# Feed-forward in seven block products twice: the second product inside the next group's first, chunk operands built in the background through DRAM

## The chip, the cores and the metric

One core of one Trainium2 chip runs the whole program. The time is the device time of one execution in microseconds; the number that counts is the median of the runs. PE is the matmul engine (PEld its weight loads), DVE the vector engine, ACT the scalar engine, POOL the GpSimd engine, SP the engine that issues most DMAs.

## What is computed

One encoder layer over 2048 + 256 tokens of 1024 channels, in float32: a mixing part (windowed attention, a Fourier mix, memory attention) that ends in an output projection with a residual add, then a squared-ReLU MLP and a final norm.

```python
    x = x + group_output_norm(y_attn, y_four, y_mem, g_grp) @ w_out
    hf = rmsnorm(x, g_ffn) @ w_ff1                      # 1024 -> 4096
    x = x + jnp.square(jax.nn.relu(hf)) @ w_ff2         # 4096 -> 1024
    ...
    return rmsnorm(x, g_final)
```

## The kernel before

Every product in float32 is done as three matmuls on reduced operands: an operand `a` is cut into a high part (`hi_of`, an ACT copy, L101) and a low part (`lo_of`, a subtraction, L104, on DVE unless POOL is named), and high x high, high x low and low x high are added up in PSUM. So each operand tile costs one ACT and one DVE (or POOL) instruction before PE can use it.

The stages follow one another: input projection (to 345 us of the profile), mixing with the output projection (to about 800 us), feed-forward (to the end). The code writes each engine's instructions in program order; a scheduler that simulates the kernel then fixes the order on every engine, with priority to what was written first, and assigns the buffers. On the chip each engine runs its list strictly in that order.

*Mixing.* 18 blocks of 128 tokens. `outproj` of a block is two halves (`op_b_0`, `op_b_1`) of 24 matmuls 512 wide through the one bank of the pool `ps_p`, each followed by a DVE add into the tile `xr`, and a store of the tile to DRAM (`X2d`). `drain(5)` lets five matmuls of it be written between the pieces of attention.

*Feed-forward.* The 2304 tokens are cut into 3 chunks of 768 (`CH`), the 4096 hidden channels into 16 groups `j` of two tiles of 128. In a group, the first product (weights `w1` x tokens `XT`) is cut into 2 x 2 blocks and done with Strassen's seven products: each (`pr`) is 12 matmuls 384 wide. Sums of weight blocks (`as`) are made on POOL, five per group, each weight operand is split by ACT and DVE (`w1h`, `w1l`), and the seven results are joined into four quarters of the hidden values (`post`: ACT copies, POOL sums, DVE adds). A DVE instruction takes the square of the ReLU, ACT and DVE split the quarter (`hh`, `hl`). The second product is plain: `slices` makes 12 pieces of 6 matmuls 512 wide (`y`), each added on DVE to `acc`. The pieces of group j - 1 are written between the products of group j (`EVEN`). ACT and POOL split `w2` (`w2h`, `w2l`).

*Chunk start.* The right operands of the seven products, `XT` (seven combinations of token halves and channel halves, high and low, one buffer), are made by `build`: it loads the mixing's result, norms it (`norm_tile`), transposes it on PE (`tf`, 48 per chunk), scales, sums and splits it. For chunks 1 and 2 this stands between the last group's `y` pieces (`tail`), after the old chunk's last `pr`; the final norm of the old chunk (`final`, L1113) runs beside the first products of the new one. Raw tiles come through a ring of 12 (`granule`).

## Time and profile before

| | |
|---|---|
| median of 3 runs | 2394.8 us (2394.55 to 2401.86) |
| profiled execution, span | 2396.3 us |
| PE busy | 2295.1 us, 12896 matmuls |
| DVE / ACT / POOL busy | 1642.2 / 1038.0 / 1035.3 us |
| DMA moved | 237.93 MB, mean 99 GB/s |

The profiled execution's own time is its span; it lies 1.5 us above the median. In the profile's groups a row gives line, engine, operation, output and inputs, shape, count, then busy time and mean duration of one, then the engine's idle time just before and what ended it. A matmul's printed duration includes its way through the pipeline, so how often PE can start one is read from neighbouring start times.

### The profile page before, as it was taken

How to read it: one execution, taken by the hardware profiler on the slowest of the kernel's cores; microseconds unless marked ns; L12 is line 12 of the kernel's file. 1: busy time of each engine (PE TensorE's matmuls, PEld its weight loads, DVE VectorE, ACT ScalarE, POOL GpSimd, SP SyncE). 2: the span in 40 equal slices, each digit the busy share in tenths (PEclk: the TensorE clock that was granted, in tenths of full speed). 3: DMA queues.
4: the chain of work that ended last, by engine and by line, in shares of the span. 5: the costliest groups of instructions: out<-in, count | busy, mean ns of one | idle time of the engine just before them, and what ended most of it. 6: DMA issues, size and time to landing. Idle time of an engine off the chain costs nothing.

```text
span 2396.3 us, 35759 instructions
## 1 busy us (share of the span) xinstructions
PE 2295.1 (96%) x12896; PEld 2072.1 (86%) x12896; DVE 1642.2 (69%) x2910; ACT 1038.0 (43%) x2406; POOL 1035.3 (43%) x1001
## 2 busy tenths in 40 slices
PE   7999978999999799999998899999998899999998
PEld 7999977888888689899996789999996789899996
DVE  6333558777666876766666996666667986666666
ACT  6433357676667633333334533233335533333333
POOL 1100130000001965555555864555556865555544
PEclk9999989999999899999999999999999999999999
DMA  7343275243333522222221432222221532222211
GB/s 245 115 146 97 72 243 211 93 143 102 111 106 102 185 71 63 70 71 71 67 66 45 159 128 67 66 71 67 71 71 53 176 106 66 71 71 67 65 50 53
DMA packets 120777, 237.93 MB, mean 99 GB/s; under 512 B 11927, under 2 KB 35479, under 8 KB 120343
## 3 DMA queue, kind: packets, MB, share of 16 engines
q1 hardware_dynamic: 111648, 219.82, 28.6%
q10 hardware_dynamic: 7191, 12.80, 1.5%
q0 software_dynamic: 1760, 3.02, 0.5%
q8 instruction: 102, 1.67, 0.3%
q14 instruction: 76, 0.62, 0.1%
HBM read 189.98 MB, written 46.53 MB: 99 GB/s over the span
## 4 chain that ended last, share of the span: by engine, by line
PE 69%; DVE 7%; POOL 4%; issue 3%; DMA 1%; ACT 1%; POOLq 0%; SPq 0%; DVEq 0%; ACTq 0%
PE y L98 27%; PE pr L98 25%; PE op L98 8%; PE ot L98 2%; PE s L98 2%; PE t L646 2%; DVE acc L1113 1%; DVE XTl L104 1%; DVE acc L295 1%; POOL w2l L104 1%; POOL as L1008 1%; DMA wos<-in_w_out_dram 1%; DVE hl L104 1%; DVE w1l L104 1%; PE sm L98 1%
## 5 line engine op out<-in xcount | busy, mean ns | idle before, releaser
L295 DVE TENSOR_TENSOR acc<-acc,y 128x512 f32<-128x512 f32 x576 | 388.8, 680 | 169.6 <-PE y L98 165.8
L98 PE MATMUL pr<-XTh,w1h 128*128 128x384 f32 x1344 | 458.1, 342 | 22.9 <-ACT w1h L101 9.7
L98 PE MATMUL y<-w2h,hh 128*128 128x512 f32 x1152 | 454.4, 394 | 20.8 <-DVE acc L295 20.7
L98 PE MATMUL pr<-XTh,w1l 128*128 128x384 f32 x1344 | 455.9, 340 | 11.5 <-DVE w1l L104 11.4
L98 PE MATMUL pr<-XTl,w1h 128*128 128x384 f32 x1344 | 456.0, 339 | 1.0 <-DVE XTl L104 1.0
L98 PE MATMUL y<-w2h,hl 128*128 128x512 f32 x1152 | 449.2, 390 | 0.7 <-DVE hl L104 0.7
L98 PE MATMUL y<-w2l,hh 128*128 128x512 f32 x1152 | 449.8, 390 | 0.0
L1008 POOL TENSOR_TENSOR as<-w,w 128x512 f32<-128x512 f32 x240 | 345.8, 1448 | 208.1 <-DVE w1l L104 171.6
L104 POOL TENSOR_TENSOR w2l<-w,w2h 128x512 fp32r<-128x512 f32 x192 | 268.9, 1422 | 365.0 <-ACT w2h L101 365.0
L101 ACT ACTIVATE w1h<-as 128x512 fp32r<-128x512 f32 x240 | 151.8, 633 | 521.5 <-PE pr L98 496.4
L104 DVE TENSOR_TENSOR w1l<-as,w1h 128x512 fp32r<-128x512 f32 x240 | 219.8, 916 | 121.4 <-ACT w1h L101 121.2
L98 PEld LDWEIGHTS pr<-XTh,w1h 128*128 128x128 f32 x1344 | 255.6, 190 | 42.0 <-ACT w1h L101 12.3
L98 PEld LDWEIGHTS pr<-XTh,w1l 128*128 128x128 f32 x1344 | 255.4, 190 | 18.9 <-DVE w1l L104 14.3
L98 PEld LDWEIGHTS y<-w2h,hh 128*128 128x128 f32 x1152 | 217.0, 188 | 59.7 <-DVE acc L295 21.6
L98 PEld LDWEIGHTS pr<-XTl,w1h 128*128 128x128 f32 x1344 | 255.7, 190 | 14.3 <-DVE XTl L104 1.7
L98 PEld LDWEIGHTS y<-w2h,hl 128*128 128x128 f32 x1152 | 216.9, 188 | 47.6 <-DVE hl L104 1.3
L98 PEld LDWEIGHTS y<-w2l,hh 128*128 128x128 f32 x1152 | 217.2, 189 | 28.8
L98 PE MATMUL pj<-hl_x,winh 128*128 128x256 f32 x720 | 204.1, 285 | 0.8 <-DVE hl_x L104 0.8
L98 PE MATMUL pj<-hh_x,winl 128*128 128x256 f32 x720 | 204.0, 284 | 0.0
L98 PE MATMUL pj<-hh_x,winh 128*128 128x256 f32 x720 | 202.9, 286 | 0.6 <-ACT hh_x L101 0.6
L127 POOL TENSOR_SCALAR stats<-stats 128x1 f32<-128x1 f32 x36 | 8.6, 239 | 394.9 <-ACT jk L747 394.9
L101 ACT ACTIVATE w2h<-w 128x512 fp32r<-128x512 f32 x192 | 119.2, 624 | 77.7 <-PE y L98 42.8
(209 smaller groups left out, 4269.6 us busy)
## 6 DMA issues: line engine op xcount, KB each, us to landing
w<-in_w_dram SPq DMA_DIRECT2D x384, 256.0 KB, 2.8
qb<-Qd SPq DMA_DIRECT2D x18, 768.0 KB, 7.4
Qd<-q SPq DMA_DIRECT2D x24, 512.0 KB, 2.8
x<-in_x_dram SPq DMA_DIRECT2D x18, 512.0 KB, 4.5
xr<-in_x_dram SPq DMA_DIRECT2D x18, 512.0 KB, 4.2
X2d<-xr SPq DMA_DIRECT2D x18, 512.0 KB, 3.1
xs<-X2d SPq DMA_DIRECT2D x36, 256.0 KB, 3.4
acc<-X2d SPq DMA_DIRECT2D x18, 512.0 KB, 5.6
```

Of the source, the lines that this page charges most:

```text
L98: pe.matmul(out, lhsT, rhs, start=start, stop=stop)
L101: act.activation(out, src, AF.Copy, scale=scale)
L104: (eng or dve).tensor_tensor(out=out, in0=src, in1=hi.bitcast(F32), op=ALU.subtract)
L127: pool.tensor_scalar(out=st, in0=st, scalar1=1.0 / width, scalar2=EPS, op0=ALU.mult, op1=ALU.add)
L295: TT(out=o, in0=a, in1=b, op=ALU.add)
L646: pe.transpose(t[:, j], p[:, j * P:(j + 1) * P], ident)
L1008: pool.tensor_tensor(out=t, in0=raw[c, j, a[0]], in1=raw[c, j, a[1]], op=a[2])
L1113: dve.scalar_tensor_tensor(out=o, in0=o, scalar=st[:, 0:1], in1=gf[n], op0=ALU.mult, op1=ALU.mult)
```

## The change

- Both products of the feed-forward are now seven block products of Winograd's form, in which sums are shared. The first keeps 7 x 12 matmuls 384 wide per group, but pairs of products add up in the same PSUM bank (`pa` to `pd`), so the results come out with fewer joins. The second works on two groups at once (`g`, halves `e`): `half_step` is 9 matmuls 512 wide, 14 of them per pair of groups (63 per group instead of 72). Its results are kept in 21 accumulators, one set for each product, which are joined only at the end of a chunk (`finish`).
- One half step is written after each product, 14 steps (`LAG`) behind: the second product of a pair of groups runs inside the first products of the next pair.
- The activations' combinations are summed on POOL (`sumA`, 4 per group) and split on ACT and DVE (`splitA`, 7 per group). The combinations of `w2` are made once, in the projection stage, on POOL with loads from POOL's own queue, and stored to DRAM (`w2_sums`, `W2T`); those of `w1` are made in chunk 0 and stored (`W1S`), and loaded again in the other chunks.
- The norm ahead of the feed-forward and its transposes go into `outproj`: behind the two `op` halves of a block come two squares on ACT, the root on POOL, one DVE scaling, and twice four transposes (`xp`) through the same one-bank pool `ps_p` with a DVE multiply each. The result goes to DRAM (`XnT`). `drain(5)` becomes `drain(6)`.
- Chunk 0's operands are built while the last blocks finish. Those of chunks 1 and 2 are built during the chunk before (`build_next`: 6 units of 8 steps, one step per product, from the third group on: 4 POOL sums, 7 ACT copies and 7 DVE subtractions of 256 elements and 14 stores per unit) and stored (`XD`). Each of the seven is loaded (`load_x`, two tiles of 0.79 MB) after the last product that reads the old one.
- The ring of raw tiles grows to 16.

```diff
+        def w2_sums():
...
+                        pool.dma_start(t, w2[2 * j + k].rearrange("p (n c) -> p n c", n=2)[:, :, qs])
...
+                    minus(t[:, 0], b[0][:, 1], b[0][:, 0])
+                    minus(t[:, 1], b[1][:, 1], t[:, 0])
+                    minus(b[0][:, 1], b[1][:, 1], b[0][:, 1])
+                    minus(b[1][:, 0], t[:, 1], b[1][:, 0])
+                    sp.dma_start(W2T[j][:, 1:3, qs], t)
+                    sp.dma_start(W2T[j][:, 3, qs], b[0][:, 1])
+                    sp.dma_start(W2T[j][:, 0, qs], b[1][:, 0])
...
             sp.dma_start(X2d[b], xt)
+            st = op.tile([P, 2], F32, tag="xst", bufs=2, name=f"xst_{b}")
+            for n in range(2):
+                jk = op.tile([P, 512], BF16, tag="xjk", bufs=1, name=f"xjk{n}_{b}")
+                act.activation(jk, xt[:, n * 512:(n + 1) * 512], AF.Square, scale=D ** -0.5, accum_out=st[:, n:n + 1])
+            rstd_of_means(st)
+            dve.tensor_scalar(out=xt, in0=xt, scalar1=st[:, 0:1], scalar2=None, op0=ALU.mult)
+            xv = xt.rearrange("p (k t) -> p k t", k=KT)
+            for n in range(2):
+                ps = ps_p.tile([P, 4, P], F32, tag="p", name=f"xp_{b}_{n}")
+                ks = slice(4 * n, 4 * n + 4)
+                for k in range(4):
+                    pe.transpose(ps[:, k], xv[:, 4 * n + k], ident)
+                    yield
+                TT(out=xv[:, ks], in0=ps, in1=gain[:, 3, ks].unsqueeze(2).to_broadcast([P, 4, P]), op=ALU.mult)
+            sp.dma_start(XnT[b], xv)
...
-            drain(5)
+            drain(6)
...
+        ORD1 = (1, 6, 2, 7, 5, 4, 3)
+        ORD2 = (1, 2, 4, 5, 6, 7, 3)
...
+        steps1 = [(c, j, i) for c in range(NCH) for j in range(NJ) for i in ORD1]
+        steps2 = [(c, g, i, e) for c in range(NCH) for g in range(NG) for i in ORD2 for e in range(2)]
+        PER = 7 * NJ
+        LAG = 14
...
+        def build_next(c):
+            for i in range(NT):
+                for kp in range(2):
+                    def put(n, src, i=i, kp=kp):
+                        t = late[0].tile([P, 2, 2, P], F32R, tag="raw", bufs=NRAW, name=f"xd_{c}_{i}_{kp}_{n}")
+                        hi_of(t[:, 0], src)
+                        lo_of(t[:, 1], src, t[:, 0])
+                        dst = XD[c, n].rearrange("q p k t -> p q k t")
+                        for q in range(2):
+                            sp.dma_start(dst[:, q, 2 * kp:2 * kp + 2, i * P:(i + 1) * P].bitcast(F32), t[:, q].bitcast(F32))
+                    yield from x_unit(c, i, kp, put)
+
+        def load_x(c, i):
+            for q, t in enumerate(xt_tiles(c, i)):
+                sp.dma_start(t.bitcast(F32), XD[c, i][q].bitcast(F32))
...
+        def half_step(r):
+            c, g, i, e = steps2[r]
...
+            for t in range(NT):
+                if e == 0:
+                    ybank[t] = ps_y.tile([P, 512], F32, tag="y", bufs=4, name=f"y_{c}_{g}_{i}_{t}")
+                ps = ybank[t]
+                ts_ = slice(t * P, (t + 1) * P)
+                mm(ps, ah[:, ts_], wh, e == 0, False)
+                mm(ps, ah[:, ts_], wl, False, False)
+                mm(ps, al[:, ts_], wh, False, e == 1)
+                if e == 1:
+                    if (c, i, t) not in acc:
+                        acc[c, i, t] = acc_tile(c, i, t)
+                        act.activation(acc[c, i, t], ps, AF.Copy)
+                    else:
+                        (sub if i == 4 else add)(acc[c, i, t], acc[c, i, t], ps)
...
+        for n in range(len(steps1) + LAG):
+            r = n - LAG
...
+            load1(n + 5)
+            load2(r + 4)
+            load_acc(r + 3)
+            split1(n + 2)
+            split2(r + 2)
+            splitA(r + 2)
+            sumA(r + 4)
+            if n < len(steps1):
+                product(n)
+                c, j, i = steps1[n]
+                if j == NJ - 1 and c + 1 < NCH:
+                    load_x(c + 1, i)
+                if n % PER == 16 and c + 1 < NCH:
+                    background = build_next(c + 1)
+                if background is not None:
+                    next(background, None)
+            if r >= 0:
+                half_step(r)
+                c, g, i, e = steps2[r]
+                if pending:
+                    pending.pop(0)()
+                if g == NG - 1 and e == 1:
+                    pending += finish(c, i)
```

How the lists of the engines change is seen at three places. A row is the engine's next instruction: line, operation, output<-inputs, width, and the engines or queues that it waits for.

DVE in the mixing, behind the add of the second `op` half of block 4 (the first row of each). Around it stand instructions of the next blocks' attention: `ptl`, `pml`, `ytl` are low parts, `p` and `stats` belong to the softmax. Before:

```order
L295 TENSOR_TENSOR xr_4_5961<-xr_4_5961,op_4_1_6061 128x512 [waits PE_49]
L104 TENSOR_TENSOR ytl_5_0_6174<-ty_5_0_6168,yth_5_0_6173 128x512 [waits Activation_49]
L637 TENSOR_REDUCE stats_6_5341<-sm_6_2_6152 128x1 [waits PE_49]
L104 TENSOR_TENSOR ytl_5_1_6183<-ty_5_1_6177,yth_5_1_6182 128x512 [waits Activation_49]
L637 TENSOR_REDUCE stats_6_5341<-sm_6_3_6191 128x1 [waits PE_49]
L104 TENSOR_TENSOR ptl_6_4_6144<-t_6_6_6201,pth_6_4_6143 128x3x128 [waits Activation_49]
```

Now:

```order
L326 TENSOR_TENSOR xr_4_6463<-xr_4_6463,op_4_1_6563 128x512 [waits PE_49]
L659 ISA p_7_0_6759,stats_7_5804<-s_7_0_6756,bias_4722,nsink_313 128x384 [waits PE_49]
L659 ISA stats_7_5804 128x1
L676 TENSOR_REDUCE stats_7_5804<-sm_6_3_6715 128x1 [waits Activation_49]
L724 RECIPROCAL stats_6_5801<-stats_6_5801 128x4
L105 TENSOR_TENSOR ptl_6_4_6653<-t_6_7_6762,pth_6_4_6652 128x3x128 [waits Activation_49]
L659 ISA p_7_1_6786,stats_7_5804<-s_7_1_6783,bias_4722,nsink_313 128x384 [waits PE_49]
L659 ISA stats_7_5804 128x1
L105 TENSOR_TENSOR pml_6_0_6795<-tm_6_0_6789,pmh_6_0_6794 128x512 [waits Activation_49]
L105 TENSOR_TENSOR pml_6_1_6816<-tm_6_1_6810,pmh_6_1_6815 128x512 [waits Activation_49]
L837 TENSOR_SCALAR xr_4_6463<-xr_4_6463,xst_4_6698 128x1024 [waits DMAHW7_49,DVE_49,Pool_49]
```

The scaling of block 4 (last row) is new; nine instructions of other work stand between the add and it, and it waits for POOL and for a DMA (the store of the tile to `X2d`).

PE in the same place, where `sm` and `s` are attention scores, `t` and `o` transposes and `otm` an attention output. Before, the matmuls behind the last of `op_4_1`:

```order
L98 MATMUL op_4_1_6061<-woh_7_4335,ytl_4_1_5958 128x512
L757 MATMUL ty_5_0_6168<-ident_60,y_5_5882 128x128 [waits DVE_49,PE_49]
L757 MATMUL ty_5_0_6168<-ident_60,y_5_5882 128x128 x3
L757 MATMUL ty_5_1_6177<-ident_60,y_5_5882 128x128 [waits DMAHW1_49,PE_49]
L757 MATMUL ty_5_1_6177<-ident_60,y_5_5882 128x128 x3
L98 MATMUL sm_6_2_6152<-km_0_4325,qb_6_5338 128x256 [waits Activation_49]
```

Now, around the second four transposes of block 4:

```order
L99 MATMUL otm_6_2_6939<-pmh_6_3_6872,vm_0_4745 128x256
L843 MATMUL xp_4_1_6712<-ident_60,xr_4_6463 128x128 [waits DVE_49]
L843 MATMUL xp_4_1_6712<-ident_60,xr_4_6463 128x128 x3
L99 MATMUL otm_6_2_6939<-pml_6_3_6873,vm_0_4745 128x256 [waits DVE_49]
L99 MATMUL otm_6_2_6939<-pmh_6_3_6872,vm_0_4745 128x256
```

The transposes stand in PE's list and wait there for DVE; everything behind them waits too.

PE at the first chunk boundary, before, where the old chunk's last `y` pieces and the new chunk's first `pr` alternate:

```order
L98 MATMUL y_0_15_0_1_14826<-w2h_0_15_1_0_14528,hh_0_15_0_14637 128x512 [waits DVE_49]
L98 MATMUL y_0_15_0_1_14826<-w2l_0_15_1_0_14529,hh_0_15_0_14637 128x512 [waits Pool_49]
L98 MATMUL y_0_15_0_1_14826<-w2h_0_15_1_0_14528,hl_0_15_0_14638 128x512
L98 MATMUL y_0_15_0_1_14826<-w2h_0_15_1_1_14532,hh_0_15_2_14368 128x512
L98 MATMUL y_0_15_0_1_14826<-w2l_0_15_1_1_14533,hh_0_15_2_14368 128x512 [waits Pool_49]
L98 MATMUL y_0_15_0_1_14826<-w2h_0_15_1_1_14532,hl_0_15_2_14369 128x512
L98 MATMUL pr_1_0_1_14937<-XTh_1_14469,w1h_1_0_1_14919 128x384 [waits Activation_49]
```

Now:

```order
L99 MATMUL pc_0_15_15476<-XTh3_0_10363,w1h_0_15_3_15464 128x384
L99 MATMUL pc_0_15_15476<-XTl3_0_10364,w1h_0_15_3_15464 128x384
L99 MATMUL pc_0_15_15476<-XTh3_0_10363,w1l_0_15_3_15465 128x384
L99 MATMUL y_0_6_3_0_15542<-w2h_0_6_3_1_15468,ah_0_6_3_1_15472 128x512 [waits Activation_49]
L99 MATMUL y_0_6_3_0_15542<-w2l_0_6_3_1_15469,ah_0_6_3_1_15472 128x512 [waits Pool_49]
L99 MATMUL y_0_6_3_0_15542<-w2h_0_6_3_1_15468,al_0_6_3_1_15473 128x512
L99 MATMUL y_0_6_3_1_15546<-w2h_0_6_3_1_15468,ah_0_6_3_1_15472 128x512
L99 MATMUL y_0_6_3_1_15546<-w2l_0_6_3_1_15469,ah_0_6_3_1_15472 128x512
L99 MATMUL y_0_6_3_1_15546<-w2h_0_6_3_1_15468,al_0_6_3_1_15473 128x512
L99 MATMUL y_0_6_3_2_15550<-w2h_0_6_3_1_15468,ah_0_6_3_1_15472 128x512
L99 MATMUL y_0_6_3_2_15550<-w2l_0_6_3_1_15469,ah_0_6_3_1_15472 128x512
```

No transpose stands there any more: the first product of chunk 1 (`pa_1_0`) follows 9 `y` matmuls behind the last product of chunk 0 (`pc_0_15`), and what it waits for is the DMA that brings its operand.

549 lines of the change are left out of this document (276 added, 273 removed).

## Prediction

> **What bounds the kernel now.** I read the profile page first (shares of the engines, the chain that ended last), then a table of busy times by stage, then the timeline of single matmuls, then the groups of instructions of an undisturbed stretch of the feed-forward.
>
> ```profile
> span 2396.3 us, 35759 instructions
> PE 2295.1 (96%) x12896; PEld 2072.1 (86%) x12896; DVE 1642.2 (69%) x2910; ACT 1038.0 (43%) x2406; POOL 1035.3 (43%) x1001
> PE 69%; DVE 7%; POOL 4%; issue 3%; DMA 1%; ACT 1%; POOLq 0%; SPq 0%; DVEq 0%; ACTq 0%
> ```
>
> The matmul engine is busy for 96% of the span and holds 69% of the chain, so matmuls taken away count nearly in full, and whatever makes PE wait counts in full too. The stages, in the order PE, PEld, DVE, ACT, POOL (busy us and instructions), clock, DMA share, GB/s:
>
> ```profile
> 345.00:772.00 427.00, 414.09 (x2448) 358.08 (x2447) 305.59 (x884) 295.92 (x869) 27.69 (x71) 0.99 0.37 128
> 1280.00:1400.00 120.00, 100.45 (x461) 84.40 (x460) 106.68 (x142) 59.65 (x138) 88.12 (x97) 0.91 0.40 134
> 1400.00:1800.00 400.00, 399.23 (x2016) 362.50 (x2014) 274.22 (x401) 129.68 (x238) 223.43 (x172) 1.00 0.22 68
> 1800.00:1940.00 140.00, 121.67 (x589) 103.31 (x590) 123.45 (x169) 67.97 (x153) 104.58 (x110) 0.96 0.37 122
> 1940.00:1960.00 20.00, 20.00 (x105) 18.39 (x104) 17.73 (x23) 7.31 (x15) 10.73 (x9) 1.00 0.30 85
> ```
>
> The mixing (345 to 772) has PE at 97%. Inside a chunk (1400 to 1800) PE never rests while DVE is 69% busy; for 20 us it even holds with DVE at 89%. At the two chunk boundaries (1280 and 1800), where the next chunk's operands are built, DVE is the full engine, 106.68 of 120 us, and PE loses time.
>
> Next the start times of neighbouring matmuls, 384 wide (pr), then 512 wide (y), and eight transposes:
>
> ```profile
> 818.24 0.34 PE L98 MATMUL pr<-XTh,w1h 128*128 128x384 f32 x1
> ...
> 818.77 0.34 PE L98 MATMUL pr<-XTh,w1h 128*128 128x384 f32 x1
> 2352.17 0.39 PE L98 MATMUL y<-w2h,hl 128*128 128x512 f32 x1
> ...
> 2352.85 0.39 PE L98 MATMUL y<-w2h,hl 128*128 128x512 f32 x1
> 781.56 1.03 PE L936 MATMUL tf<-ident,xs 128*128 128x128 f32 x8
> ```
>
> Three steps each: (818.77 - 818.24)/3 = 0.177 us and (2352.85 - 2352.17)/3 = 0.227 us. A group (two ff tiles of one chunk) is 84 pr and 72 y: 31.2 us, 0.200 us per matmul.
>
> **The change, part by part.** *Removed matmuls.* The second product takes 63 instead of 72 y matmuls in each of 48 groups: 432 x 0.227 = **-98 us**; a group is then 29.1 us. pr stays at 84. 144 tf transposes go and 144 xp come, at 0.13 us each: zero, though 96 of them move from the boundaries into the mixing.
>
> *Boundaries.* Of 461 matmuls in 1280 to 1400, 48 are tf (6 us) and 413 x 0.200 = 83 us the rest: 31 of 120 us were lost. For 1800 to 1940 (589): 108 + 6, 26 lost. Together 57. The new order puts the next chunk's first product directly behind the last one of the old, so this loss goes; what is late next is the finish of the chunk. It adds 12 POOL adds, 12 DVE adds and 12 DVE scalings in the 14 half steps (58 us) that end a chunk:
>
> ```profile
> L295 DVE TENSOR_TENSOR acc<-acc,y 128x512 f32<-128x512 f32 x151 | 101.9, 680 | 44.7 <-PE y L98 43.6
> L1008 POOL TENSOR_TENSOR as<-w,w 128x512 f32<-128x512 f32 x64 | 89.8, 1410 | 60.9 <-DVE w1l L104 57.0 <-DMA w<-in_w_dram 3.7
> L104 POOL TENSOR_TENSOR w2l<-w,w2h 128x512 fp32r<-128x512 f32 x50 | 68.4, 1389 | 109.4 <-ACT w2h L101 109.4
> L104 DVE TENSOR_TENSOR w1l<-as,w1h 128x512 fp32r<-128x512 f32 x67 | 59.9, 894 | 38.1 <-ACT w1h L101 38.1
> L104 DVE TENSOR_TENSOR hl<-m,hh 128x384 fp32r<-128x384 f32 x36 | 33.8, 938 | 1.2 <-ACT hh L101 1.2
> L295 DVE TENSOR_TENSOR m<-m,pr 128x384 f32<-128x384 f32 x39 | 20.4, 545 | 2.1 <-PE pr L98 1.6 <-POOL md L1055 0.5
> L1055 POOL TENSOR_TENSOR mx<-mx,m 128x384 f32<-128x384 f32 x13 | 18.1, 1392 | 0.9
> L1113 DVE SCALAR_TENSOR_TENSOR acc<-acc,ff,gf 128x512 f32<-128x512 f32 x12 | 17.7, 1518 | 0.8 <-POOL ff L132 0.8
> ```
>
> (The last row is from 1280 to 1400.) DVE: 12 x 0.894 + 12 x 1.518 = 29 us on top of two groups. The two groups alone cost DVE 46 us (next paragraph), so 75 us of work meet 58 us of matmuls. I take 14 us lost per boundary, nearly the excess of 17, because some scalings run on into the next group; bounds 0 (all of them do) and 28 (the loss of before). Term: -57 + 28 = **-29**.
>
> *DVE and POOL inside the groups.* Before, 12.8 groups in the 400 us: 21.4 us of DVE each. Now per group 9.75 instead of 12 adds of y (the rest goes to ACT as copies or vanishes), -1.5; 7 instead of 4 low halves of the activations (384 wide, 0.94), +2.8; five instead of four adds of pr, +0.5. That is 23.2 of 29.1 us, 80%. The background build adds 42 low halves of 256 elements to some 7 groups of each of the first two chunks, at about 0.6 (half to two thirds of the 512 wide row): +3.6, 92%. POOL: 7 x 1.39 for w2l and 4 x 1.39 for sums of the activations, 15 us; in chunk 0 four weight sums (1.41) more, 21 us, 72%. At 89% DVE the old kernel lost nothing, at 89% with POOL at 73% it lost a quarter. I take 2 us for each of chunk 0's seven groups with the build, 3 in its rest, 4 in chunk 1: **+21**, bounds 0 and 65 (16% of 14 groups, the lost share of 1280 to 1400).
>
> The reason it could be more is that DVE and POOL hinder each other:
>
> ```profile
> 1510.65 0.69 DVE L104 TENSOR_TENSOR w1l<-w,w1h 128x512 fp32r<-128x512 f32 x1 [0.33 <-ACT w1h L101]
> 1512.07 2.55 POOL L104 TENSOR_TENSOR w2l<-w,w2h 128x512 fp32r<-128x512 f32 x2 [7.67 <-ACT w2h L101]
> 1527.16 0.56 DVE L104 TENSOR_TENSOR hl<-mx,hh 128x384 fp32r<-128x384 f32 x1 [1.54 <-ACT hh L101]
> 1527.73 2.87 POOL L104 TENSOR_TENSOR w2l<-w,w2h 128x512 fp32r<-128x512 f32 x2 [1.52 <-ACT w2h L101]
> 1528.23 1.21 DVE L104 TENSOR_TENSOR hl<-m,hh 128x384 fp32r<-128x384 f32 x1
> 1529.51 1.63 DVE L104 TENSOR_TENSOR w1l<-w,w1h 128x512 fp32r<-128x512 f32 x1
> ```
>
> With POOL idle a w1l takes 0.69 and an hl 0.56; beside a w2l they take 1.63 and 1.21. Adds of y, with one input in PSUM, stay at 0.68 on average. The Trainium skill, "SBUF — State Buffer", section "Who interferes with whom", says that a DVE instruction with two SBUF inputs contends with a GpSimd instruction that reads SBUF, and that the later one blocks fully. By it the sum would be the third rival's; the rows agree in the kind of instruction, and w1l ends 0.54 us behind the pair, but hl ended (1529.44) 0.3 us behind the middle of the pair, in less than its own 0.56.
>
> *Mixing.* Each of 18 blocks gets, behind its second op product: two ACT squares, POOL's root, a DVE scaling of 1024, four transposes, a DVE multiply, four transposes through the same single PSUM bank, another multiply.
>
> ```profile
> L295 DVE TENSOR_TENSOR xr<-xr,op 128x512 f32<-128x512 f32 x31 | 21.2, 685 | 27.5 <-PE op L98 27.5
> L747 ACT ACTIVATE jk<-y 128x512 bf16<-128x512 f32 x16 | 10.1, 631 | 3.8 <-DVE y L681 3.1
> L128 POOL TENSOR_TENSOR stats<-stats,mhalf 128x1 f32<-128x1 f32 x30 | 16.5, 549 | 2.5
> L749 DVE TENSOR_SCALAR y<-y,stats 128x512 f32<-128x512 f32 x15 | 7.3, 484 | 14.3 <-POOL stats L128 13.3 <-ACT pm L638 1.1
> ```
>
> The bare chain to the first transpose is 0.69 + 2 x 0.63 + 0.55 + 2 x 0.48 = 3.5 us, and in DVE's order nine other instructions stand in it, at the stage's mean (305.59/884 = 0.35) 3.1 us. The order puts 5.5 to 6 us of other matmuls (its rows, each at its width's time) over these 6.6: 0.8 short. Between the two halves stand 2.3 us of matmuls against eight such DVE instructions and the multiply, 3.5 us: 1.2 short. Between the second half and the next op product stand 1.6 to 2.9 us against nine and the multiply, 3.8: 1.6 short. That is 3.6 us per block, 65 in all, if DVE is never ahead; it has 28% free, so 0 is the other bound. I take the middle, 1.9 us per block, **+34**.
>
> *The rest.* The w2 sums in the projection stage (128 POOL instructions, 64 loads from POOL's queue, 96 stores from SP's) stand in POOL's queue ahead of the root for later norms: **+4**, bounds 0 and 15 (a few loads waited for). At the end of the mixing op_17_1, both xp and only then the first product stand in a row, so one bare chain (3.5) is exposed: **+3**, 0 to 10. In the tail, the last 14 half steps run without products, 28.6 us of matmuls, over 14 w2l, 12 sums and some six more on POOL (about 40 us) and 41 us of DVE; and three adds, norms and stores follow the last matmul, where before 8 us follow (2388.39 to 2396.3):
>
> ```profile
> 2388.00 0.39 PE L98 MATMUL y<-w2h,hl 128*128 128x512 f32 x1
> ```
>
> I take **+18**, bounds 5 and 35. The operand loads at a boundary are 14 tiles of 0.79 MB beside the weights, on SP's queue, each waiting for the product that last reads its buffer, with weight loads queued behind it. The fastest stretch moved
>
> ```profile
> 350.00:360.00 10.00, 7.52 (x41) 6.81 (x41) 6.83 (x29) 6.93 (x27) 0.00 (x0) 0.66 0.98 372
> ```
>
> 372 GB/s: 11 MB take 30 us, with weights 40 us, against 29 us of products; the 11 us behind are covered by the weights' lead of four to five steps (16 us or more). Zero, bound +50.
>
> Sum: -98 - 29 + 21 + 34 + 4 + 3 + 18 = -47, from the profiled 2396.3 to 2349. The median of the runs, 2394.8, lies 1.5 lower, so **2348 us**.
>
> **Rivals.** *PE stays full.* 89% of DVE with a full PE speaks for it, and each instruction of the xp chain may run ahead. Then mixing 0, groups 0, boundaries -57 + 10, tail +8, rest +7: -98 - 47 + 15 = -130, **2265** for the median. Against it: the 97% in the mixing, with one PSUM bank now shared by twice the users.
>
> *The mixing is not covered.* 3.6 us per block instead of 1.9: **2379**.
>
> *DVE and POOL take turns* (the other side). If every POOL instruction excludes every DVE one with two SBUF inputs, a group needs their sum: POOL 15, DVE 7 x 0.69 + 7 x 0.56 + 4 x 0.55 = 11, together 26 of 29.1, but 31.6 in chunk 0, and with the build 4.8 more (24 POOL sums at 0.7 and 42 low halves at 0.4, over 7 groups). Place: chunk 0's 16 groups, 9 x 2.5 + 7 x 7.3 = 74, chunk 1's build 7 x 1.7 = 12, boundaries +10 and tail +17 (towards their upper bounds), less the 21 counted: +92, **2440**. It decides from 29.1 us per group on. Before, the same sum is 17.4 + 9 = 26 of 31.2, which fits with its full PE, so nothing in the trace excludes it; against it speaks the hl at 1528. By the Trainium skill's page "SBUF — State Buffer" this is the expected course.
>
> *Operand loads come late* by most of 30 us at each boundary: 2348 + 50 = **2398**, no change.
>
> **Chances.** My forecast 0.42, PE full 0.20, mixing uncovered 0.15, turns 0.15, late loads 0.08. About 0.3% (7 us) is what a measurement here can tell. Faster: the first three, 0.77; same 0.08; slower 0.15. The range 2268 to 2428 leaves out half of the full-PE case and half of the turns; the likeliest case alone spans 2320 to 2375.
>
> **What would show it.** y matmuls 3024 instead of 3456. Inside chunk 2 a group in 29 to 29.5 us; in chunk 0 more, with DVE near 90% and PE waiting for low halves. At the boundaries no idle stretch over some us ended by an operand load. In the mixing, idle time ahead of xp and of op released by DVE. The forecast is wrong if chunk 0's groups take over 31 us (turns) or if the mixing stays at 97%.

## The result, and the profile after

The changed kernel takes 2422.7 us (median of 4 runs, 2420.2 to 2425.8) against 2394.7 us of the kernel before in the same comparison: a ratio of 1.0113, 95% interval 1.0092 to 1.0134. It is 28 us slower, where the prediction had 47 us faster. The profiled execution spans 2424.1 us, 27.8 us more than that of before. The page's busy times and the chain that ended last:

```profile
PE 2248.1 (93%) x12464; PEld 2015.8 (83%) x12464; DVE 1819.9 (75%) x3068; ACT 1132.5 (47%) x2661; POOL 1184.4 (49%) x1141
PE 40%; DVE 8%; DMA 3%; issue 2%; POOL 2%; ACT 1%; SPq 0%; ACTq 0%; POOLq 0%; DVEq 0%
```

PE has 432 matmuls less and is busy 47 us less, yet the span is longer: PE's share falls from 96% to 93%, and its part of the chain from 69% to 40%. To find where, the span is cut at landmarks that both kernels have: the start of the last `pj` matmul (input projection), the first and last `s` (scores), the first product of the feed-forward and the last `y` matmul, each from the timeline of PE.

| stretch | before | after | difference |
|---|---|---|---|
| start to first `s` | 344.5 | 376.8 | +32.2 |
| first `s` to last `s` (mixing) | 419.4 | 437.4 | +18.0 |
| last `s` to first product (transition) | 46.0 | 82.8 | +36.8 |
| first product to end | 1586.4 | 1527.1 | -59.3 |

The feed-forward did get faster; the three stretches ahead of it lost 87 us. The same stretches by stage, before and then after (stretch and its length, then busy us and instructions of PE, PEld, DVE, ACT and POOL, clock, DMA share, GB/s):

```profile
40.00:340.00 300.00, 298.81 (x2516) 298.43 (x2514) 136.56 (x296) 121.90 (x306) 37.02 (x79) 1.00 0.40 124
345.00:764.00 419.00, 406.09 (x2401) 351.50 (x2400) 299.66 (x865) 290.57 (x852) 26.20 (x67) 0.99 0.37 127
764.00:810.00 46.00, 36.92 (x194) 28.91 (x192) 37.44 (x70) 35.81 (x94) 30.93 (x56) 0.93 0.45 152
```

```profile
40.00:340.00 300.00, 278.22 (x2285) 274.73 (x2284) 128.00 (x250) 105.95 (x249) 161.25 (x239) 0.98 0.66 212
377.00:814.00 437.00, 417.73 (x2468) 356.80 (x2469) 319.97 (x898) 296.67 (x902) 38.15 (x94) 0.99 0.38 136
814.00:897.00 83.00, 51.86 (x224) 40.03 (x222) 46.82 (x91) 29.68 (x89) 33.26 (x44) 0.79 0.43 146
1000.00:1160.00 160.00, 147.12 (x697) 127.05 (x695) 139.85 (x184) 64.29 (x136) 114.77 (x90) 0.98 0.59 176
1200.00:1400.00 200.00, 200.00 (x1007) 181.90 (x1006) 174.64 (x229) 85.15 (x164) 140.73 (x102) 1.00 0.57 187
1420.00:1460.00 40.00, 33.26 (x153) 27.93 (x151) 40.00 (x47) 19.97 (x46) 33.05 (x28) 0.96 0.54 165
1480.00:1660.00 180.00, 169.01 (x810) 149.69 (x809) 147.87 (x213) 80.53 (x171) 97.81 (x79) 0.97 0.64 186
2000.00:2320.00 320.00, 320.00 (x1611) 291.62 (x1610) 260.15 (x365) 134.60 (x253) 156.81 (x122) 1.00 0.42 127
```

*Projection* (first row): 231 matmuls fewer in the same 300 us, at 8.42 per busy us (2516/298.81) 27.4 us. Of these 20.6 are idle time of PE (298.81 - 278.22); the other 6.8 are lost while PE counts as busy, with the mean clock at 0.98 instead of 1.00. POOL is busy 161 instead of 37 us, DMA moves 212 instead of 124 GB/s.

*Mixing and transition*: 120 of the 144 `xp` fall into the mixing (15.6 us at 0.13), and the last 48 `op` matmuls (10.9 us at 0.227) have slipped out of it behind the last `s`. So the mixing lost 18.0 - 15.6 + 10.9 = 13 us, and the transition, which has these `op` and 24 `xp` (3.1) more and 48 `tf` (6.2) less, 36.8 - 10.9 - 3.1 + 6.2 = 29 us.

*Feed-forward*: in chunk 2 (2000 to 2320) PE is full, 320/1611 = 0.199 us per matmul, so a group of 147 takes 29.2 us (before: 400/2016 in the prediction's row, so 30.95 us for 156). The same holds in chunk 0 without the build (1200 to 1400). With the build (1000 to 1160 and 1480 to 1660) 697 of 806 and 810 of 906 matmuls run. At the boundary (1420 to 1460) 153 of 201 run while DVE has no idle time at all. From the last product to the last `y` pass 42.6 us, for 135 matmuls that take 30.9 at the full rate (0.229 us each), so 12 are lost, and from there to the end 25 us. Before it was 47.9 us for 204 matmuls (46.3, so 2 lost), and 8.

### The profile page after: what moved, and what is told of

Read it like the earlier page. It is cut to its first block, busy times and chain, and to the rows that moved or that the text cites. A ratio compares the mean times of both kernels' runs of the same rounds, so it can differ in the third digit from the quotient of the medians.

```text
span 2424.1 us, 37193 instructions
## 1 busy us (share of the span) xinstructions
PE 2248.1 (93%) x12464; PEld 2015.8 (83%) x12464; DVE 1819.9 (75%) x3068; ACT 1132.5 (47%) x2661; POOL 1184.4 (49%) x1141
## 4 chain that ended last, share of the span: by engine, by line
PE 40%; DVE 8%; DMA 3%; issue 2%; POOL 2%; ACT 1%; SPq 0%; ACTq 0%; POOLq 0%; DVEq 0%
PE y L99 20%; PE pb L99 6%; PE pa L99 6%; PE pc L99 6%; PE pd L99 3%; DVE acc L326 2%; DMA XD<-xd 2%; DVE al L105 1%; DVE w1l L105 1%; DVE m L1093 1%; DVE xd L105 1%; POOL w2l L105 1%; DMA R<-XnT 0%; DVE m L326 0%; DVE x L326 0%
## 5 line engine op out<-in xcount | busy, mean ns | idle before, releaser
L105 POOL TENSOR_TENSOR w2l<-w,w2h 128x512 fp32r<-128x512 f32 x336 | 471.7, 1406 | 483.8 <-ACT w2h L102 455.1
L99 PE MATMUL y<-w2l,ah 128*128 128x512 f32 x1008 | 399.1, 397 | 22.2 <-POOL w2l L105 22.0
L99 PE MATMUL y<-w2h,al 128*128 128x512 f32 x1008 | 395.4, 394 | 2.7 <-DVE al L105 2.7
L99 PE MATMUL y<-w2h,ah 128*128 128x512 f32 x1008 | 379.6, 397 | 12.2 <-DVE acc L326 6.3
L105 DVE TENSOR_TENSOR w1l<-w,w1h 128x512 fp32r<-128x512 f32 x304 | 286.6, 943 | 15.9 <-ACT w1h L102 15.2
L105 DVE TENSOR_TENSOR al<-m,ah 128x384 fp32r<-128x384 f32 x240 | 210.7, 879 | 105.6 <-ACT ah L102 98.4
L102 ACT ACTIVATE w1h<-w 128x512 fp32r<-128x512 f32 x304 | 190.0, 625 | 168.8 <-PE pa L99 51.0
L99 PEld LDWEIGHTS y<-w2l,ah 128*128 128x128 f32 x1008 | 190.9, 189 | 52.6 <-POOL w2l L105 30.0
L99 PEld LDWEIGHTS y<-w2h,ah 128*128 128x128 f32 x1008 | 190.4, 190 | 41.9 <-DVE acc L326 11.6
L99 PEld LDWEIGHTS y<-w2h,al 128*128 128x128 f32 x1008 | 190.7, 189 | 39.2 <-DVE al L105 3.6
```

What stands on the lines that cost most here:

```text
L99: pe.matmul(out, lhsT, rhs, start=start, stop=stop, skip_group_check=more)
L102: act.activation(out, src, AF.Copy, scale=scale)
L105: (eng or dve).tensor_tensor(out=out, in0=src, in1=hi.bitcast(F32), op=ALU.subtract)
```

## The experiments

Most of these kernels were run once; their times are compared with the 2422.7 us of the change, whose own four runs span 5.6 us, so a smaller difference of totals says nothing. Where a ratio stands, it is against the kernel before, run beside it. "Last `pj`" is the landmark for the projection: 339.1 us before, 369.1 after. Kernels in which the projection is written alike gave 368.8 to 372.0 for it, so differences of 3 us are not read.

### What the chunk builds cost

`e4_no_build` leaves the build out; chunks 1 and 2 use chunk 0's operands.

```diff
-                    load_x(c + 1, i)
-                if n % PER == 16 and c + 1 < NCH:
-                    background = build_next(c + 1)
+                    XT[c + 1, i] = XT[c, i]
```

> The background build and the operand loads are left out; chunks 1 and 2 multiply with chunk 0's operands (the output differs). Theory (the build fills DVE where it has no room): chunk 0 from 475 to about 440 to 445 us, chunk 1 from 504 to about 482 to 487, chunk 2 unchanged, the run 50 to 60 us shorter, 2362 to 2372. Rival (DVE and POOL take turns, so that chunk 0's weight sums alone keep PE waiting): chunk 0 stays above 465.

`e5_spread` keeps the build but takes a step in every second run of eight products only, so it lasts twice as long.

```diff
-                if background is not None:
+                if background is not None and n % PER // 8 % 2 == 0:
```

> The background build runs 8 steps, rests 8 steps, and so on: the same instructions over 88 steps of a chunk instead of 48. Theory (the loss is DVE over its capacity in the groups with the build): chunk 1, whose other groups leave DVE 20% free, loses 10 to 20 us less, chunk 0, where the weight sums already hold DVE at 90%, only 5 to 10 less; the run 2395 to 2410. Rival (a build step costs PE the same wherever it stands): 2418 to 2426.

Measured: e4 2376.9 us, -46 (5 us above its range); e5 2397.8 us, -25, as expected. By the start times of the products, chunk 0 takes 475.4 us in the change, 447.2 in e4 and 462.6 in e5, chunk 1 504.0, 482.3 and 487.8: the build costs 28 and 22 us. Their stretch 1000 to 1160, first e4, then e5:

```profile
1000.00:1160.00 160.00, 160.00 (x807) 145.60 (x806) 144.25 (x183) 67.27 (x128) 118.13 (x85) 1.00 0.45 138
```

```profile
1000.00:1160.00 160.00, 158.55 (x794) 143.19 (x794) 149.51 (x193) 70.48 (x141) 124.50 (x95) 1.00 0.52 161
```

Without the build PE is full at DVE 90% and POOL 74% (144.25 and 118.13 of 160), which the turns rival had at 31.6 us per group. At the boundaries 14 us are lost each time without the build and its operand loads, and with them no more at the second (the group that ends it takes 45.1 against 44.9 us; at the first, where the next build starts in it, 47.4 against 45.2), and PE waits there for no operand load: these loads cost nothing, as predicted. Half the density gives back half of the loss.

What the build holds up is read from the waits of 1000 to 1160 (who waits for what, us in total, times, longest), of the change and then of e5:

```profile
ACT xd L102 <- DMA XD<-xd: 29.3, 8, 9.0
ACT xd L102 <- DVE w1l L105: 21.5, 8, 5.2
DVE xd L105 <- ACT xd L102: 19.5, 13, 6.9
```

```profile
DVE xd L105 <- ACT xd L102: 2.6, 4, 1.2
```

The build's tiles (`xd`) come from the ring of 16 raw tiles, beside the weights. ACT's copy into a new one waits until an older tile of the ring has been stored or split; DVE's low part stands in DVE's list and waits for the copy, and the adds and low parts on which PE depends stand behind it. So DVE's 160 us are spent: 139.85 busy and 19.5 waiting for these copies. In e5 DVE waits 2.6 us instead, and PE is full with DVE busy for longer (149.51). That the store of `xd` holds a place in the chain that ended last of the page, 2% as "DMA XD<-xd", fits with it. Both parts, DVE's load and its waiting, become smaller in e5; a ring of its own for the build, which would separate them, wasn't tried.

`e8_no_w1_sums` leaves out four POOL sums per group of chunk 0 (raw blocks of `w1` are used instead).

```diff
-                ptt(s1, a21, a22, ALU.add)
-                ptt(s2, s1, a11, ALU.subtract)
-                ptt(a21, a11, a21, ALU.subtract)
-                ptt(a12, a12, src1.pop((0, j, "s2")), ALU.subtract)
```

> The four weight sums per group that POOL makes in chunk 0 are left out (raw blocks are stored and used in their place, so the output differs); DVE's instructions are the same in number. Theory A (POOL's instructions lengthen DVE's): in chunk 0 the square falls from 1.13 to about 0.9 us and the loss to the build from 29 to under 19 us. Theory B (DVE's count alone): the loss stays within 5 us of 29.

Measured: 2399.1 us, -24. By the start times, 15 us of it lie in the eight groups of chunk 0 with the build, whose loss falls from 29 to 14 us, as theory A had it; 6 lie in chunk 0's first group, where nothing is built. DVE's groups in 1000 to 1160, first of the change, then of e8 (line, engine, operation, shapes, count, busy us, mean ns):

```profile
L105 DVE TENSOR_TENSOR al<-m,ah 128x384 fp32r<-128x384 f32 x24 | 24.8, 1035 | 0.0
L105 DVE TENSOR_TENSOR w1l<-w,w1h 128x512 fp32r<-128x512 f32 x24 | 23.3, 971 | 0.0
L1093 DVE SCALAR_TENSOR_TENSOR m<-m 128x384 f32<-128x384 f32 x17 | 19.3, 1137 | 0.0
L105 DVE TENSOR_TENSOR xd<-R,xd 128x256 fp32r<-128x256 f32 x20 | 15.6, 781 | 14.6 <-ACT xd L102 14.5
```

```profile
L105 DVE TENSOR_TENSOR w1l<-w,w1h 128x512 fp32r<-128x512 f32 x36 | 35.1, 976 | 1.8 <-ACT w1h L102 1.8
L1090 DVE SCALAR_TENSOR_TENSOR m<-m 128x384 f32<-128x384 f32 x20 | 20.2, 1009 | 0.0
L105 DVE TENSOR_TENSOR al<-m,ah 128x384 fp32r<-128x384 f32 x24 | 17.4, 726 | 3.1 <-ACT ah L102 3.1
L105 DVE TENSOR_TENSOR xd<-R,xd 128x256 fp32r<-128x256 f32 x20 | 13.1, 654 | 17.9 <-ACT xd L102 17.9
```

With less on POOL most of the same DVE instructions are shorter: `al` 0.73 instead of 1.04 us, the square 1.01 instead of 1.14 (0.9 was expected), the `xd` of `R` 0.65 instead of 0.78; `w1l` did not change. That alone isn't the gain: in e5 `al` and `w1l` are as long as in the change (1.03 and 1.04 us) under a full PE. The sums also held two tiles of the ring per group, and ACT's wait for the store of `xd` falls from 29.3 to 15.7 us in e8; the two effects are not separated. The Trainium skill, "SBUF — State Buffer", section "Who interferes with whom", says that a DVE instruction with two SBUF inputs contends with a GpSimd instruction that reads SBUF, under an exclusive lock. `al`, the square and `xd` have two such inputs and agree in the kind; `w1l` has two as well and does not show it. Full blocking, by which the prediction's rival had 31.6 us for a group of chunk 0, does not agree with the 29.2 measured there without the build.

`e6_square_act` moves the square of one quarter in each group from DVE to ACT.

```diff
-                act.activation(M[11], ps, AF.Copy)
-                square(M[11])
+                act.activation(M[11], ps, AF.Relu)
+                act.activation(M[11], M[11], AF.Square)
```

> One of the four squares per group (that of M11) goes from DVE to ACT (a Relu in place of the copy, then a Square): DVE loses 48 instructions of 0.97 us, ACT gains 48 of 0.5. Theory (DVE is the bound in the groups with the build, at the boundaries and in no others): 12 to 25 us faster, 2397 to 2410; the groups that take 29.2 us stay at that. Rival (POOL's w2l or the DMAs hold PE): within 5 us of 2422.

Measured: 2416.3 us, -6; a miss in size, and hardly more than the spread of the runs. By the start times chunk 0 became 4.6 us shorter, chunk 1 2.2, and chunk 2, where nothing is built, 2.3 at its boundary; in 1000 to 1160 DVE still waits 18.9 us for ACT's copies. Taking one DVE instruction of 0.97 us out of each group brings little of PE's time back.

### What the handover to the feed-forward costs

`e3_late_xp` writes the norm and the `xp` of the last two blocks behind both blocks' `op` matmuls.

```diff
-            [norm, transposes and store, in outproj]
+            if b >= NBLK - 2:
+                late_norm.append(outnorm(b, xt))
+                if b == NBLK - 1:
+                    feed.extend(late_norm)
+            else:
+                yield from outnorm(b, xt)
```

> The norm and transposes of the last two blocks (16, 17) are written behind both blocks' output products, nothing else. Theory (PE's list: op_17 stands behind xp_16, and xp_16 waits 15 us for DVE, which has 42 low parts of chunk 0's operands ahead of it): the first product starts 8 to 18 us earlier than 897 us, the run falls to 2404 to 2414. Rival (chunk 0's operands themselves are late, not the order): the first product stays at 893 to 900 us.

Measured: 2412.1 us, -11; the first product starts at 885.6 instead of 897.0, both as expected. What it removed is seen in PE's timeline of the change (start, duration, what; in brackets the idle time before and what ended it), and the rows ahead of the waits, POOL's root and DVE's scaling for block 16 and DVE's scaling for block 17:

```profile
866.53 1.12 PE L843 MATMUL xp<-ident,xr 128*128 128x128 f32 x4 [15.00 <-DVE xr L837]
873.88 1.12 PE L843 MATMUL xp<-ident,xr 128*128 128x128 f32 x4 [6.23 <-DVE xr L845]
876.43 0.63 PE L99 MATMUL op<-wol,yth 128*128 128x512 f32 x1
876.86 0.63 PE L99 MATMUL op<-woh,ytl 128*128 128x512 f32 x1
...
894.30 1.12 PE L843 MATMUL xp<-ident,xr 128*128 128x128 f32 x4 [4.28 <-DVE xr L837]
...
896.97 0.67 PE L99 MATMUL pa<-XTh,w1h 128*128 128x384 f32 x1
```

```profile
861.90 0.74 POOL L137 TENSOR_TENSOR xst<-xst,mhalf 128x1 f32<-128x1 f32 x1
865.74 0.74 DVE L837 TENSOR_SCALAR xr<-xr,xst 128x1024 f32<-128x1024 f32 x1
...
893.49 0.75 DVE L837 TENSOR_SCALAR xr<-xr,xst 128x1024 f32<-128x1024 f32 x1 [2.75 <-DMA X2d<-xr]
```

PE waits 15.0 and 6.2 us in front of block 16's transposes, with 48 `op` matmuls of block 17 behind them in its list, ready. The building of chunk 0's operands holds this norm up in two lists. Block 16's squares are done at 855.8 us; POOL's root comes at 862.6, behind sums for the operands, and DVE's scaling at 865.7, behind 32 of their 42 low parts since 847. Behind the stall an `op` starts every 0.43 us (876.43, 876.86) instead of 0.23, up to 879.8: the clock is part of the price. The last chain, 889.6 to 897.0, is exposed as predicted, but at 7 us instead of 3.5: the scaling works in place and waits for the store of the tile (2.75 us).

### What the `w2` sums cost in the projection

`e2_no_w2_sums` leaves them out (raw blocks of `w2` are used).

```diff
-        w2_work = w2_sums()
+        w2_work = iter(())
```

> The sums of w2 are left out altogether (no loads, POOL sums or stores in the projection stage; the second product takes plain blocks of w2 in their place, so the output differs). Both theories: the last pj comes back to 339 to 341 us, the run falls by about 30 us to 2392. If it does not, the stage is slower for another reason.

Measured: 2397.1 us, -26 (5 us short of what was expected); last `pj` 340.3, as expected. So all of the projection's loss comes with these sums. Three further kernels leave parts of them out. `e9_no_pool_sums` keeps loads and stores, without the four subtractions:

```diff
-                    minus(t[:, 0], b[0][:, 1], b[0][:, 0])
-                    [and the other three]
-                    sp.dma_start(W2T[j][:, 1:3, qs], t)
+                    sp.dma_start(W2T[j][:, 1:3, qs], b[0])
```

> The w2 sums' four POOL subtractions per set are left out, their loads (POOL's queue) and stores (SP's queue) stay, in bytes and number (the stored blocks are raw ones, so the output differs). If the traffic costs the projection stage its 30 us, the last pj stays within 6 us of 369; if POOL's arithmetic and what waits for it does, the last pj comes to 339 to 350.

`e15_loads_only` drops the three stores as well, and `e16_arith_only` keeps the subtractions alone, on three fixed tiles.

> The 64 loads of raw w2 stay in POOL's list; the four subtractions and the three stores of each set are left out (the feed-forward uses raw w2 blocks, so the output differs). Theory A (the stores on SP's list and POOL's waits between loads and sums make the chain, loads alone are harmless): last pj at 340 to 345, total 2397 to 2402. Theory B (16.8 MB more read traffic delays the token loads and the norm): last pj at 352 to 360, total 2408 to 2416. With nothing of the sums last pj was at 340.3, with loads and stores but no arithmetic at 360.8, with all at 369.1.

> The 128 subtractions stay in POOL's list, on three tiles that are filled once; no loads and no stores of the sums (the feed-forward uses raw w2 blocks, so the output differs). If POOL's time itself delays the norm's root: last pj at 348 to 352 (the 8 to 10 us that leaving the arithmetic out gave back), total 2404 to 2410. If the arithmetic costs only because it waits for the loads: last pj at 340 to 344, total 2397 to 2401.

Measured: last `pj` 340.3 with nothing, 359.1 with the loads, 360.8 with loads and stores, 369.1 with all: +19, +2, +8. (Totals 2414.1 for e15, 2409.9 for e9, 2405.5 for e16.) e9 lies between its two expectations. e16 came to 358.4 and met neither of its own, by a way of its own: without loads to wait for, 40 of the 128 subtractions stand in the first 45 us, and all of its loss lies ahead of 57 us, so it doesn't price the arithmetic where the change has it. e15 came where its theory B, the traffic, had put it. But POOL computes nothing for `w2` there, and the way of its longest stall can be read in POOL's list:

```profile
130.04 0.72 POOL L213 DMA_DIRECT2D w2r<-in_w_dram  x1 [2.10 <-DMA w2r<-in_w_dram]
...
134.99 0.72 POOL L213 DMA_DIRECT2D w2r<-in_w_dram  x1 [0.71 <-DMA w2r<-in_w_dram]
...
136.05 0.56 POOL L133 TENSOR_TENSOR st_m<-st_m,mhalf 128x1 f32<-128x1 f32 x1
```

The square that this `st_m` needs was done at 126.6. POOL first issues loads, each of which waits until an earlier load into the same buffer has landed; PE's transposes come 7.2 us late, of the 19 that the loads cost. This is the mechanism that the prediction named, the root behind POOL's queue. But it isn't the only one. In the change itself the waits of 20 to 340 us read (who waits for what, us in total, times, longest):

```profile
POOL w2r L213 <- DMA W2T<-w2r: 65.6, 18, 13.2
ACT jk_x L163 <- DMA Kd<-ks: 31.5, 5, 12.3
```

A load waits for the store of the sums that were in its buffer, and that store, on SP, waits for POOL. Behind it in SP's list stand the stores of `K`, whose buffer the square `jk_x` of a later norm takes over. The longest of these waits, in SP's and ACT's lists:

```profile
278.50 0.33 SPq L224 DMA_DIRECT2D W2T<-w2r  x1
278.93 2.54 SPq L413 DMA_DIRECT2D Kd<-ks  x4
285.54 1.06 ACT L163 ACTIVATE jk_x<-x 128x1024 bf16<-128x1024 f32 x1 [12.28 <-DMA Kd<-ks]
```

The tile of `K` was ready at 272.2, but its stores stand behind that of the sums, which POOL finished at 278.5; PE waits 5.6 us for this norm. Transfers also land later: between 20 and 340 us a token load takes 7.1 us from issue to landing instead of 4.3 in e2, a store of `K` 3.8 instead of 2.4 (medians), so traffic may have a part in each link.

Five kernels each took one link away:

`e1_sp_loads` issues the raw loads on SP instead of POOL:

> The w2 sums' 64 loads are issued from SP's queue instead of POOL's; the rest as in the changed kernel. Theory 1 (POOL's own queue: it waits for stores and landings of these tiles while the root for the next norm stands behind): the projection stage, whose last pj is at 369 us against 339 before, ends 10 to 25 us earlier, the run falls from 2422 to about 2400 to 2412. Rival (the traffic itself: DMA share 0.84 against 0.4): the last pj stays within 5 us of 369.

`e7_pool_stores` issues the three stores on POOL instead of SP:

> The stores of the w2 sums go to POOL's queue, the loads stay there: SP's queue is as before the change. Theory (on SP the stores of the sums wait for POOL, the stores of K behind them come late, and the square of the next norm waits for the buffer that they read): the last pj at 340 to 355 us instead of 369, the run 15 to 29 us faster. Rival (traffic): the last pj within 5 us of 369.

`e11_in_place` makes the sums in place (two tiles per set, two stores) and loads one set ahead:

> The w2 sums are made in place (two tiles per set instead of three, two stores instead of three), and a set's loads are issued one set ahead of its sums. If waits on landings and on buffers in POOL's and SP's lists are the cost, the last pj comes to 345 to 360 us and the run to 2398 to 2414; if the traffic is, the last pj stays within 5 us of 369.

`e12_jk_moved` gives the squares' scratch tile another buffer:

```diff
-                jk = apool.tile([P, D], BF16, tag="Ks", bufs=1, ...)
+                jk = fpool.tile([P, D], BF16, tag="Mh", bufs=2, ...)
```

> In the projection stage the square's scratch tile (jk) takes another buffer than K's staging tile (ks); nothing else differs from the changed kernel. Theory (a chain: SP holds the store of ks behind the stores of the w2 sums, jk waits for that store, POOL's root and DVE's scaling follow, PE waits for the transposes): the last pj falls from 369 to 340 to 355 us, the run by 14 to 29 us to 2393 to 2408. Rival (POOL's list itself, or the traffic): the last pj stays above 362.

`f9_root_off_pool` makes the root without POOL (on top of the edits of f8, below):

```diff
-                rstd_of(st, D)
+                dve.tensor_scalar(out=st, in0=st, scalar1=1.0 / D, scalar2=EPS, op0=ALU.mult, op1=ALU.add)
+                act.activation(st, st, AF.Sqrt)
+                dve.reciprocal(out=st, in_=st)
```

> The four edits of f8_no_jk, and the root of the token norms in the projection stage is made on ACT and DVE (a DVE scale and add, an ACT square root, a DVE reciprocal) instead of POOL. Theory (the root stands in POOL's list behind the loads and sums of w2, so the norm waits for them whatever they wait for; e15 and e16 each lost 18 us by it): last pj at 340 to 350 instead of 372, total 2340 to 2350. Rival (traffic, buffers or SP's list hold the token norms): last pj at 365 to 375, total 2362 to 2372.

| kernel | last `pj` | total |
|---|---|---|
| after | 369.1 | 2422.7 |
| e1_sp_loads | 371.1 | 2418.2 |
| e7_pool_stores | 363.8 | 2449.9 |
| e11_in_place | 376.4 | 2430.7 |
| e12_jk_moved | 373.3 | 2426.1 |
| f9_root_off_pool (f8: 372.0) | 377.0 | 2375.3 (f8: 2368.3) |

None of the five gave the loss back: e7's last `pj` is 5 us earlier, the others' are as late or later, and e1 and e12 came where their rivals (traffic; POOL's list or traffic) had put them. But to take a single link away is not a clean test. The scheduler builds every list anew for each kernel, and the traces show another link in its place. In e12 the squares of a norm are done at 143.9, but the root comes at 153, behind a subtraction that waits for a store of the sums, and PE waits 6.3 us:

```profile
147.89 0.71 POOL L217 TENSOR_TENSOR w2s<-w2r 128x256 f32<-128x256 f32 x1 [5.14 <-DMA W2T<-w2r]
```

In f9, where POOL no longer makes the root, the squares wait for the stores of `K`, 40.6 us in total and up to 13.1 at a time (10 to 380 us).

e7's total is longer for another reason: its first `s` starts at 415.7 us instead of 376.8. With the stores gone, SP's list was built in another order, and eight loads of the output weights came ahead of the first `qb`, which was issued at 407.91 and for which PE's first scores wait:

```profile
366.18 34.32 SPq L811 DMA_DIRECT2D wos<-in_w_out_dram  x8
```

What stays open: whether taking the root off POOL and moving the squares' buffer together would give the 29 us back, and how much of it is plain traffic. No kernel here tests either.

### The edits together

`f4_four_fixes` joins late xp, spread build, square on ACT and the in-place sums; `f6_with_jk` has the moved buffer instead of the in-place sums; `f7_with_tail` adds to f6 that DVE makes the low parts of `w2` in every second half step of the last pair of groups; `f8_no_jk` is f7 without the moved buffer.

```diff
-                lo_of(l, s, h, pool)
+                lo_of(l, s, h, dve if c == NCH - 1 and g == NG - 1 and e == 1 else pool)
```

> The changed kernel with the late norm of blocks 16 and 17 (-11 alone), the build spread over 88 steps (-26 alone), one square on ACT (-8 alone) and the w2 sums in place one set ahead (unknown, -25 to 0). If the four losses are separate, the sum is 2378 less the last term: 2353 to 2380, faster than before by 0.6 to 1.7%. If they cover one another (square and spread both free DVE), up to 2390.

> The late norm, the spread build, the square on ACT and the moved jk, without the sums in place: 2378 less what the moved jk brings. By the theory 2350 to 2364; by the rival 2370 to 2378. In both cases faster than before.

> As f6, and in the last pair of groups every second low part of w2 is made on DVE instead of POOL. In the tail POOL is busy for 38 of 40 us and DVE for 27, so the end comes 3 to 8 us earlier than in f6; if DVE and POOL only hinder each other there, no change within 3 us.

> Late xp, spread build, square on ACT and the tail's low parts on DVE, without the moved buffer of the squares. If the moved buffer gained nothing (as it did alone): 2366 to 2371, as f7_with_tail's 2369.7. If it gained the 2.6 us by which f6 and f4 differ: 2371 to 2374.

| kernel | us | ratio to before | interval |
|---|---|---|---|
| f4 | 2377.3 | 0.9923 | 0.9906 to 0.9940 |
| f6 | 2374.7 | 0.9913 | 0.9896 to 0.9929 |
| f7 | 2369.7 | 0.9895 | 0.9880 to 0.9909 |
| f8 | 2368.3 | 0.9892 | 0.9876 to 0.9909 |

f4 lies at the upper end of its range and f6 where the rival had it: neither the sums in place nor the moved buffer adds to the other three edits, and f8, without the moved buffer, agrees. f7's 5 us against f6 are as expected, though their runs overlap (2370.4 to 2378.7 and 2368.9 to 2374.1). f8 is 26 us faster than the kernel before and 54 faster than the change, with the projection's 30 us still lost. The tail's edit shortened last product to last `y` from 42.6 us (f6) to 40.1 (f8).

## Why the prediction was wrong

By its own terms (us); the measured column uses the landmarks, the matmuls lost and the chunks' lengths in e4 as above.

| term | predicted | bounds | measured |
|---|---|---|---|
| matmuls removed | -98 | | -84 (30.95 to 29.2 us per group) |
| boundaries | -29 | -57 to -1 | -28 (14 to 15 us lost at each) |
| DVE and POOL in the groups | +21 | 0 to 65 | +50 |
| mixing | +34 | 0 to 65 | +13 |
| `w2` sums in the projection | +4 | 0 to 15 | +32 |
| end of the mixing | +3 | 0 to 10 | +29 |
| tail | +18 | 5 to 35 | +27 (10 + 17) |
| operand loads | 0 | 0 to 50 | 0 |
| sum | -47 | | +39; the spans differ by 27.8 |

The 11 us between the sum and the spans lie in a place for which the prediction has no term: by the start times of its matmuls, the feed-forward of before lost about 22 us outside its boundaries and its tail, that of now 8.

What remains at a boundary and the loads came as predicted. The sign was lost in two small terms, which missed their own upper bounds, and a third that was sized too low; the largest term was 14 us too large.

*The `w2` sums, +4 (failed, 28 us).* The step "stand in POOL's queue ahead of the root for later norms" named a real chain, and e15 shows it. Its size was put at "a few loads waited for". It left out that each load waits for a buffer, that a buffer comes free only by a store on SP which itself waits for POOL, and that SP's list holds stores and loads on which the norms depend: a loop through two in-order lists. It also counted idle time alone; 6.8 of 27.4 us in 40 to 340 us are lost while PE counts as busy. How the loss divides among the links and the traffic stays open.

*The end of the mixing, +3 (failed, 26 us).* The step priced one bare chain at the very end. It left out the transposes of block 16: they stand in PE's list ahead of 48 ready `op` matmuls, while POOL and DVE build chunk 0's operands, so neither is at the stage's mean there. e3 gave back 11 of the 29 us. In e3 PE still waits 4.8 and 3.6 us for the adds of `op` halves and 3.9 us for the last scaling; the rest wasn't separated.

*DVE and POOL in the groups, +21 (29 us too small).* The term priced DVE's instructions, the low part at 0.6 us (it measures 0.78 in 1000 to 1160), and came to 92%; DVE is busy for 87% (139.85 of 160). It counted no waiting inside DVE's list: 19.5 of 160 us, for copies that wait for the ring. So the sum of busy times could not show it. Of the 21 us predicted, 14 fell on chunk 0's groups with the build (measured 28), 3 on the rest of chunk 0 (its groups behind the build lose nothing) and 4 on chunk 1 (measured 22); all of the 50 us belong to the build (e4).

*Mixing, +34 (21 us too large, and not by the wait that it named).* The step let PE wait for DVE in front of `xp` and of the next `op`. This is what PE idles there in 377 to 814, and in front of `s` (line, engine, operation, shapes, count, busy us, mean ns, idle us and what ended it); the last row is `s` before, 345 to 764:

```profile
L843 PE MATMUL xp<-ident,xr 128*128 128x128 f32 x120 | 18.1, 273 | 0.0
L99 PE MATMUL op<-woh,yth 128*128 128x512 f32 x240 | 95.8, 399 | 0.1
L99 PE MATMUL s<-kb,qb 128*128 128x384 f32 (+1 forms) x286 | 71.6, 355 | 15.8 <-DVE stats L659 8.2 <-DMA qb<-Qd 7.3
L98 PE MATMUL s<-kb,qb 128*128 128x384 f32 (+1 forms) x287 | 75.0, 354 | 13.1 <-DVE stats L620 7.8 <-DMA qb<-Qd 5.2
```

In front of `xp` and `op` PE hardly waits: here the chain runs ahead, as the rival "PE stays full" had it. PE is busy 95.6% of the stage (417.73/437), before 96.9%; it idles 6.4 us more than before, in front of `s`, `o` and other attention matmuls. Where the other half of the 13 us comes from stays open.

*Matmuls removed, -98 (14 us too large).* A group takes 29.2 us as predicted, but before it took 30.95, not 31.2: the step of 0.177 us was read at 818 us. In the full stretch of before a 384 wide matmul starts every 0.174 us, now every 0.177 (ten steps each):

```profile
1499.80 0.34 PE L98 MATMUL pr<-XTl,w1h 128*128 128x384 f32 x1
...
1501.54 0.34 PE L98 MATMUL pr<-XTh,w1l 128*128 128x384 f32 x1
2099.83 0.34 PE L99 MATMUL pb<-XTl,w1h 128*128 128x384 f32 x1
...
2101.60 0.34 PE L99 MATMUL pb<-XTh,w1l 128*128 128x384 f32 x1
```

The 512 wide ones start every 0.229 instead of 0.227 us. Over 4032 and 3024 matmuls this is about 15 us. Why they are slower isn't shown; the granted clock reads 1.00 in both stretches.

*The rivals.* Chunk 0's groups with the build took up to 38 us, over the 31 that the prediction gave as the sign of turns; but DVE and POOL taking turns fell with e4 and with chunk 0's second half, where PE is full. "PE stays full" holds for chunk 2, for groups without the build and, ahead of `xp` and `op`, for the mixing. The case that came about, small handovers ahead of the feed-forward that cost more than the products gain, wasn't among them.

## What to carry to other kernels

Work that "fits beside" a full engine has to be checked in each in-order list that it enters, DMA lists included: follow what the moved instruction waits for, then what stands behind it, around the whole loop. At the seam between two stages an engine's load is that of both stages; take it from the list at that place, not from a stage's average. The step between matmuls that a price rests on belongs to the stretch that it prices. A background task that shares a ring of buffers with the main work can make the main work's engines wait for its buffers; half its density over twice the stretch was a cheap edit (here -25 us).

## What the runs showed of the hardware that was not expected

After a wait of several microseconds PE comes back at about half its rate for some 4 us, so a stall costs more than its length. In e15's projection PE's rows around the stall, 256 wide, and a stretch of 10 us behind it (columns as above):

```profile
137.55 0.66 PE L181 MATMUL tp_m<-ident,m 128*128 128x128 f32 x2 [7.18 <-DVE m L165]
138.44 0.41 PE L99 MATMUL pj<-hh_x,winl 128*128 128x256 f32 x1
138.65 0.41 PE L99 MATMUL pj<-hh_x,winh 128*128 128x256 f32 x1
...
141.91 0.28 PE L99 MATMUL pj<-hl_x,winh 128*128 128x256 f32 x1
142.03 0.28 PE L99 MATMUL pj<-hh_x,winl 128*128 128x256 f32 x1
```

```profile
140.00:150.00 10.00, 10.00 (x80) 10.00 (x79) 6.96 (x14) 4.60 (x11) 0.94 (x2) 0.92 0.43 144
```

The wait is 7.2 us. Up to 141.6 a matmul starts every 0.21 us, then every 0.12. PE counts as busy throughout, and yet 80 matmuls run from 140 to 150, at a mean clock of 0.92, against 88 in the ten behind. In the transition, behind waits of 15 and 6 us, the slow steps last from 875.9 to 879.8, and the mean clock of its 83 us is 0.79.
